# An expert MLP: which engine awaits the ring's stores, and which engine evicts which block of the last expert

## The chip, the core and the metric

The kernel runs on one core of a Trainium2 chip. A core has five engines that run side by side, each with its own instruction stream: TensorE (PE, matrix products), VectorE (DVE), ScalarE (ACT), GpSimd (POOL) and SyncE (SP, which computes nothing and here issues transfers and hands out permissions). They meet only through semaphores: an instruction waits until a semaphore has reached a value, and adds to one when it is done. Transfers between HBM and the on-chip memory are issued by an engine, run on 16 shared DMA engines, and add 16 to a semaphore as they land. TensorE writes its products to PSUM, from where VectorE or ScalarE copy ("evict") them to SBUF.

The metric is the device time of one execution in microseconds. The median of three runs of the kernel before is 181.86 us (181.73 to 181.88).

## The reference

Eight experts, each a two-layer perceptron on 256 rows of its own:

```python
n_experts, capacity, hidden, expert_hidden = 8, 256, 512, 2048
h = np.matmul(x, w1) + b1[:, np.newaxis, :]
h = np.maximum(h, 0)
return (np.matmul(h, w2) + b2[:, np.newaxis, :]).astype(np.float32)
```

x is 8x256x512, w1 8x512x2048, w2 8x2048x512, all float32; the output is 8x256x512 float32.

## The kernel before

The kernel works in float16 with float32 sums. Almost all of it lies in one section whose instruction order and semaphores are written by hand (it opens at line 138 and closes at line 324; the instructions that close it carry line 138 in the profile). Its steps s run from 0 to 10. In step s the first layer of expert s is computed (line 292, hidden units in 16 blocks of 128, each evicted with bias and ReLU by ScalarE, line 226), and the second layer of expert s - 3 (lines 309 and 314: first the bias b2 as a product with a row of ones, then 16 products summed in PSUM). The second layer's 256 rows are two row blocks, tb = 0 and tb = 1, computed one after the other. TensorE adds to `s_po` as each is finished.

`evict(e, tb)` (line 197) copies a finished row block of expert e from PSUM to `results[e]`, and adds to `s_out[tb]`. ScalarE's program (lines 216 to 234) calls it for tb = 0, behind the activations of its step; VectorE's program (lines 210 to 214) calls it for tb = 1, behind the transposes of the next expert's input. For the last expert, E - 1 = 7, in step 10, neither engine has other work left.

The results are stored in three ways:

- Experts 0 to 3 and experts 4 and 5 are stored as two groups by GpSimd, in `flush` (line 165). These are the ring's stores: 2 MB and 1 MB, the last two transfers that GpSimd issues, on the queue on which it also loads all weights. Their landing adds to `landed["out0"]` and `landed["out4"]`.
- Expert 6 is stored by SyncE (line 265) in the last step, between the two permissions for the last expert's weights.
- Expert 7 is stored by SyncE (line 269) when both of its row blocks are evicted (lines 267 and 268). Both of SyncE's stores add to `s_last`.

SyncE's program ends with waiting for the ring's two landings (lines 270 and 271). Then the section is closed: SyncE posts that it has come to the end (line 138), every engine answers with a DRAIN or a NOP and a post, SyncE awaits these and, by a NOP behind the section (line 325), `s_last`, that is, the landing of its own stores. After that the program's end (line 353, where the context that holds the kernel is left) has every engine DRAIN, and all five meet in a barrier that GpSimd opens; a second, short one follows, and the program is over. An engine other than SyncE goes on to its DRAIN of line 353 as soon as it has answered SyncE's post.

Of the kernel before, what the change touches and what calls it, by code (L numbers as in the profile page):

```python
# [10 lines left out]
def kernel(  # L11
# [12 lines left out]
    nc = tc.nc  # L24
# [4 lines left out]
    E, T, H = x.shape  # L29
# [9 lines left out]
    LAG = 3  # L39
    NW = 3  # L40
    NPH = 4
    GROUPS = {0: 4, 4: 2}
# [41 lines left out]
    landed = {}  # L84
# [19 lines left out]
    def transposes(e):  # L104
        t, p0, R = x16[e]
        n = R // nTB
        if e >= 2:
            first = max(f for f in X_LOADS if f <= e)
            nc.vector.wait_ge(landed[f"x{first}"], 16)
            nc.vector.wait_ge(s_ph, nJ * (e - 1))  # L110
        mine = xT[:, e % 2 * nKC * T : (e % 2 + 1) * nKC * T].rearrange("p (kc t) -> p kc t", kc=nKC)
        last = None
        for g in range(T // R // B):
            src = t[p0 + B * g : p0 + B * (g + 1)]
            for b in range(nB):
                block = src[:, :, b * (H // nB) : (b + 1) * (H // nB)].rearrange(
                    "p (n tb) (i kc) -> p tb kc n i", tb=nTB, kc=nKC)
                dst = mine[b * B : (b + 1) * B].rearrange(
                    "p kc (tb g i n) -> p tb g kc n i", tb=nTB, i=B, n=n)
                if n == 1:  # L120
                    last = nc.vector.transpose(out=dst[:, :, g, :, 0, :], in_=block[:, :, :, 0, :])  # L121
                    continue
                for tb in range(nTB):
                    last = nc.vector.transpose(out=dst[:, tb, g], in_=block[:, tb])  # L124
        return last
# [4 lines left out]
        out=b1_rows[:], in_=b1.rearrange("e (b i) -> (e b) i", b=nB)))  # L130
# [59 lines left out]
    for b in range(nB):  # L190
        turned = nc.vector.transpose(  # L191
            out=b1T[b * B : (b + 1) * B, nB - 1 - b : nB - 1 - b + nJ * B],
# [2 lines left out]
    turned.then_inc(s_b1, 1)  # L195

    def evict(e, tb):
        engine = nc.vector if tb else nc.scalar
        copy = nc.vector.tensor_copy if tb else nc.scalar.copy
        first, n = group_of.get(e, (e, 1))  # L200
        rows = P // n
        at = (e - first) * rows
        engine.wait_ge(s_po, nTB * e + tb + 1)
        for k in range(n):
            bank = (e % 2 * nTB + tb) * H
            last = copy(out=results[e][at : at + rows, k * nTB + tb, :],  # L206
                        in_=po[k * rows : (k + 1) * rows, bank : bank + H])
        last.then_inc(s_out[tb], 1)

    for s in range(E + LAG):  # L210
        if s + 1 < E:
            transposes(s + 1).then_inc(s_xT, 1)
        if s >= LAG:
            evict(s - LAG, 1)

    nc.scalar.wait_ge(s_b1, 1)
    for s in range(E + LAG):
        if s < E:
            split = group_of.get(s, (s, 1))[1]
            if s > LAG:  # L220
                nc.scalar.wait_ge(s_po, nTB * (s - LAG))
            for j in range(nJ):
                mine = hT[:, s % (LAG + 1) * nJ * T : (s % (LAG + 1) + 1) * nJ * T]
                bias_at = j * B + s * nB + nB - 1
                nc.scalar.wait_ge(s_ph, nJ * s + j + 1)
                nc.scalar.activation(  # L226
                    out=mine.rearrange("p (tb j k i) -> p j tb k i", tb=nTB, j=nJ, k=split)[:, j],
                    in_=ph[:, j % NPH, 0:T].rearrange("p (tb i k) -> p tb k i", tb=nTB, k=split),
                    func=relu,
                    bias=b1T[:, bias_at : bias_at + 1],  # L230
                    scale=1.0,
                ).then_inc(s_credit, 1)
        if s >= LAG:
            evict(s - LAG, 0)

# [4 lines left out]
    def store(e, p0, p1, engine):  # L242
        dst = out[e].rearrange("(p r) h -> p r h", r=nTB)
        engine.dma_start(out=dst[p0:p1], in_=results[e][p0:p1]).then_inc(s_last, 16)

    for s in range(E + LAG):
# [5 lines left out]
        e = s - LAG  # L252
# [14 lines left out]
    for tb in range(nTB):  # L267
        nc.sync.wait_ge(s_out[tb], E)
    store(E - 1, 0, P, nc.sync)
    for first in GROUPS:  # L270
        nc.sync.wait_ge(landed[f"out{first}"], 16)


    nc.tensor.sem_inc(s_credit, NPH)
# [83 lines left out]
```

## Time and profile before

| what | value |
|---|---|
| time, median of 3 runs | 181.86 us |
| the profiled execution's own time | 182.14 us |
| its span, first to last instruction | 180.4 us |
| TensorE busy (matmul) | 134.9 us, 75% of the span |
| VectorE, ScalarE, GpSimd busy | 86.8, 75.6, 12.5 us |
| mean DMA rate over the span | 224 GB/s |
| granted TensorE clock, mean | 0.970 |

Reading help: PE is TensorE, PEld its weight loads, DVE VectorE, ACT ScalarE, POOL GpSimd, SP SyncE. A "q" behind an engine (SPq, POOLq) marks its sequencer, which handles waits, posts, branches and the issue of transfers; such instructions are not counted as busy. L206 is line 206 of the kernel. "x" before a tile's name, as in `x<-po`, is the tile of the last two experts' results: they lie in buffers that held inputs before. Times in the views are from the start of the span; the views by source line give starts to a tenth of a microsecond and lengths in ns.

### The profile page before, as it was taken

The numbers are of one execution on the slowest core, as the hardware profiler recorded it, in microseconds if no ns is written. First come the engines' busy times: TensorE is split into PE (matmuls) and PEld (weight loads), VectorE is DVE, ScalarE is ACT, GpSimd is POOL, SyncE is SP. The second block draws the span as 40 slices with busy tenths as digits, with TensorE's granted clock in tenths as the row PEclk, the third lists the DMA queues.
The fourth block names the chain that finished last, engine by engine and source line by source line (L and its number), as shares of the span: only waits on it lengthen the run. The fifth ranks groups of instructions, "written<-read, shape, count | busy, mean of one in ns | idle before, by whom it ended". The sixth has DMA issues, their size and how long they took to land. (4 is left out here: it accounts for less than half of the span.)

```text
span 180.4 us, 2999 instructions
## 1 busy us (share of the span) xinstructions
PE 134.9 (75%) x784; PEld 92.5 (51%) x784; DVE 86.8 (48%) x124; ACT 75.6 (42%) x153; POOL 12.5 (7%) x27
## 2 busy tenths in 40 slices
PE   0004969868688970998978896889688979996960
PEld 0003869868688430794378544864388434442320
DVE  1989929585000399996099807990510020201010
ACT  3201777757588040492557352763188010110100
POOL 6000021020200010001010001000200011010000
PEclk9999999999999998599999999999999999999995
DMA  5998999999899999989999999999899999999994
GB/s 229 251 229 180 233 229 205 207 229 227 185 233 202 234 203 233 225 185 229 229 214 196 233 225 203 211 229 225 189 229 229 211 207 215 220 218 172 380 422 169
DMA packets 3826, 40.46 MB, mean 224 GB/s; under 512 B 448, under 2 KB 464, under 8 KB 1392
## 3 DMA queue, kind: packets, MB, share of 16 engines
q0 software_dynamic: 3200, 38.28, 96.2%
q1 hardware_dynamic: 576, 2.10, 2.9%
q10 hardware_dynamic: 48, 0.07, 0.1%
q14 instruction: 2, 0.02, 0.0%
HBM read 71.39 MB, written 4.19 MB: 419 GB/s over the span
## 5 line engine op out<-in xcount | busy, mean ns | idle before, releaser
L292 PE MATMUL ph<-xT,w_sb 128*128 x512 | 72.3, 302 | 33.1 <-PEq L277 30.1
L292 PEld LDWEIGHTS ph<-xT,w_sb 128*128 x512 | 66.7, 146 | 39.7 <-issue 31.0
L226 ACT ACTIVATE hT<-ph,b1T 128x256 f16<-128x256 f32 x128 | 60.2, 475 | 47.1 <-PE ph L292 43.6
L124 DVE STREAM_TRANSPOSE xT<-x 32x256 f16<-32x256 f16 (+1 forms) x64 | 52.8, 893 | 25.2 <-DMA x<-in_x_dram 22.1
L314 PE MATMUL po<-w_sb,hT 128*128 x256 | 58.1, 380 | 0.0
L314 PEld LDWEIGHTS po<-w_sb,hT 128*128 x256 | 24.4, 97 | 29.5 <-issue 4.0
L206 DVE COPY out<-po 32x512 f32<-32x512 f32 (+1 forms) x20 | 13.7, 687 | 42.6 <-PE po L314 42.4
L206 ACT COPY out<-po 32x512 f32<-32x512 f32 (+1 forms) x20 | 11.5, 577 | 28.7 <-PE po L314 28.5
L88 POOL DMA_DIRECT2D w_sb<-in_w_dram x18 | 9.7, 544 | 137.4 <-PE po L314 71.3
L121 DVE STREAM_TRANSPOSE xT<-x 32x256 f16<-32x256 f16 x32 | 14.0, 436 | 0.5
L309 PE MATMUL po<-b_sb,ones 1*128 x16 | 6.1, 383 | 6.2 <-issue 3.6
L206 DVE COPY x<-po 128x512 f32<-128x512 f32 x2 | 1.4, 692 | 15.3 <-PE po L314 15.3
L309 PEld LDWEIGHTS po<-b_sb,ones 1*128 1x128 f16 x16 | 1.4, 90 | 12.0 <-issue 12.0
L206 ACT COPY x<-po 128x512 f32<-128x512 f32 x2 | 1.2, 586 | 15.3 <-PE po L314 15.3
L191 DVE STREAM_TRANSPOSE b1T<-b_rows 32x512 f32<-32x512 f32 x4 | 4.1, 1026 | 0.5 <-issue 0.5
L135 ACT CAST x<-x 128x1024 f16<-128x1024 f32 x1 | 1.0, 1044 | 3.2 <-DMA x<-in_x_dram 3.2
L133 DVE CAST x<-x 128x1024 f16<-128x1024 f32 x1 | 0.7, 695 | 3.0 <-DMA x<-in_x_dram 3.0
L88 POOL DMA_DIRECT2D out_dram<-out x2 | 1.1, 538 | 9.2 <-DVE out L206 9.2
L128 ACT ACT_TABLE_LOAD x1 | 1.3, 1283 | 0.7 <-PEq L342 0.7
L88 POOL DMA_DIRECT2D x<-in_x_dram x2 | 1.1, 550 | 0.0
L127 DVE MEMSET ones<- 1x128 f16 x1 | 0.2, 165 | 0.9 <-PEq L342 0.9
L88 POOL DMA_DIRECT2D b_sb<-in_b_dram x1 | 0.5, 509 | 0.0
(5 smaller groups left out, 0.7 us busy)
## 6 DMA issues: line engine op xcount, KB each, us to landing
w_sb<-in_w_dram POOLq DMA_DIRECT2D x14, 2048.0 KB, 41.2
w_sb<-in_w_dram POOLq DMA_DIRECT2D x2, 1536.0 KB, 22.5
out_dram<-out POOLq DMA_DIRECT2D x1, 2048.0 KB, 25.3
x<-in_x_dram SPq DMA_DIRECT2D x2, 512.0 KB, 3.8
x<-in_x_dram POOLq DMA_DIRECT2D x1, 1024.0 KB, 34.6
w_sb<-in_w_dram POOLq DMA_DIRECT2D x2, 512.0 KB, 24.7
out_dram<-out POOLq DMA_DIRECT2D x1, 1024.0 KB, 18.5
out_dram<-x SPq DMA_DIRECT2D x2, 512.0 KB, 6.6
```

Source lines behind the costliest of these rows:

```text
L88: engine.dma_start(**kw).then_inc(landed[key], 16)
L121: last = nc.vector.transpose(out=dst[:, :, g, :, 0, :], in_=block[:, :, :, 0, :])
L124: last = nc.vector.transpose(out=dst[:, tb, g], in_=block[:, tb])
L128: tc.keep_in_program_order(nc.scalar.activation(out=warm[:], in_=ones1[:], func=relu))
L133: nc.vector.tensor_copy(out=x16[0][0][:], in_=x32[0][:])
L135: tc.keep_in_program_order(nc.scalar.copy(out=x16[1][0][:], in_=x32[1][:]))
L191: turned = nc.vector.transpose(out=b1T[b * B : (b + 1) * B, nB - 1 - b : nB - 1 - b + nJ * B], in_=b1_rows[:].rearrange("r (i j) -> r j i" ...
L206: last = copy(out=results[e][at : at + rows, k * nTB + tb, :], in_=po[k * rows : (k + 1) * rows, bank : bank + H])
L226: nc.scalar.activation(out=mine.rearrange("p (tb j k i) -> p j tb k i", tb=nTB, j=nJ, k=split)[:, j], in_=ph[:, j % NPH, 0:T].rearrange("p ...
L292: last = nc.tensor.matmul(ph[:, j % NPH, 0:T], w1_sb[:, bass.ds(w_from + (kc * M + j), P, nJ)], xT[:, bass.ds(x_at + kc * T, T)], start=(k ...
L309: nc.tensor.matmul(bank, ones1[:], b2_sb[:, bass.ds(s * H, H)], start=True, stop=False)
L314: last = nc.tensor.matmul(bank, hT[:, bass.ds(t * (nJ * P // H) + j * P, P)], w2_sb[:, bass.ds(w_at + j * H, H)], start=False, stop=(j == ...
```

## The change

Two edits. The waits for the ring's two landings move from the end of SyncE's program to the end of ScalarE's. And the last expert's two evictions exchange engines: VectorE copies tb = 0, ScalarE tb = 1; for the other experts nothing changes. SyncE still waits for both row blocks before it stores the last expert.

```diff
     def evict(e, tb):
-        engine = nc.vector if tb else nc.scalar
-        copy = nc.vector.tensor_copy if tb else nc.scalar.copy
+        by_vector = tb == (0 if e == E - 1 else 1)
+        engine = nc.vector if by_vector else nc.scalar
+        copy = nc.vector.tensor_copy if by_vector else nc.scalar.copy
...
         if s >= LAG:
-            evict(s - LAG, 1)
+            evict(s - LAG, 0 if s - LAG == E - 1 else 1)
...
         if s >= LAG:
-            evict(s - LAG, 0)
+            evict(s - LAG, 1 if s - LAG == E - 1 else 0)
+    for first in GROUPS:
+        nc.scalar.wait_ge(landed[f"out{first}"], 16)
...
     store(E - 1, 0, P, nc.sync)
-    for first in GROUPS:
-        nc.sync.wait_ge(landed[f"out{first}"], 16)
```

All instructions keep their place and number on VectorE, GpSimd and TensorE; on ScalarE and SyncE only the two waits before the section's closing branch change sides.

## The prediction

> **What bounds the kernel now.** The change touches the last expert and the end of the program, so I read the chain of waits there first, from 165.9 us on (start, length, work), and beside it the page's first line:
>
> ```profile
> span 180.4 us, 2999 instructions
> ...
> 165.81 0.20 issue
> ...
> 170.62 3.57 PE po L314 x16
> 174.20 0.02 issue
> 174.22 0.69 DVE x L206
> ```
>
> TensorE's matmuls of the last expert's second row block end at 174.20. VectorE's eviction follows until 174.91, and there the chain stops. What fills the 5.5 us to 180.4 is no computing, so the page's shares say nothing about it. I went on with the waits of SyncE from 174 us (total, times, longest):
>
> ```profile
> SPq L268 <- DVE x L206: 6.1, 1, 6.1
> SPq L271 <- DMA out_dram<-out: 2.0, 1, 2.0
> SPq L353 <- PEq L353: 1.5, 2, 1.1
> SPq L138 <- DMA out_dram<-x: 0.7, 1, 0.7
> ```
>
> SyncE (SP) waits for the eviction, then 2.0 us at line 271 for a ring store, then only 0.7 us at line 138 for its own last store. After that it waits once more, for 1.1 us, in the barrier that ends the program (L353). So somebody reaches that barrier 1 us later than SP. The views by source line name it (engine, operation, count, length min/median/max in ns, first and last start):
>
> ```profile
> L271 SPq EVENT_SEMAPHORE  x1: 17/17/17, 177.4 to 177.4; - x1
> ...
> L88 SPq COMPARE_BRANCH  x1: 33/33/33, 177.4 to 177.4; - x1
> ...
> L138 SPq EVENT_SEMAPHORE  x4: 17/22/735, 177.6 to 177.9; - x4
> L138 ACTq DRAIN  x1: 8/8/8, 177.6 to 177.6; - x1
> L138 POOLq NOP  x1: 13/13/13, 177.6 to 177.6; - x1
> ...
> L138 SPq NOP  x1: 13/13/13, 178.7 to 178.7; - x1
> ...
> L353 POOLq DRAIN  x1: 1929/1929/1929, 177.7 to 177.7; - x1
> L353 SPq DRAIN  x1: 7/7/7, 178.8 to 178.8; - x1
> L353 POOLq EVENT_SEMAPHORE  x1: 17/17/17, 179.7 to 179.7; - x1
> ```
>
> The hand-written section is closed at line 138 by a post of SP at 177.6, on which every engine waits. GpSimd (POOL) gets it at 177.6, leaves the section and starts the program's closing DRAIN at 177.7. That takes 1.929 us, to 179.63. SP is ready at 178.8, held to then by the landing of its last store. The barrier therefore opens at 179.7, by POOL's DRAIN, 0.9 us after SP stood there. **The bound of the end is this chain: ring store lands, SP closes the section, POOL drains.** The store of the last expert, which one would suspect, ends 0.9 us too early to matter.
>
> **The change part by part.**
>
> *The waits for the ring stores leave SP.* Two waits and the branch behind them stay in number and go to ScalarE (ACT). The rows of the two issues in question, from the views by line and of transfers:
>
> ```profile
> L244 SPq DMA_DIRECT2D out_dram<-x x1: 344/344/344, 175.0 to 175.0; - x1
> ...
> DMA to landing us min/median/max: 3.6/3.6/3.6
> ...
> 158.83 0.54 POOL L88 DMA_DIRECT2D out_dram<-out  x1 [8.94 <-DVE out L206]
> ...
> out_dram<-out POOLq DMA_DIRECT2D x1, 1024.0 KB, 18.5
> ```
>
> The later ring store lands at 158.83 + 18.5 = 177.3; SP's wait passes it on at 177.4. The last store is issued at 175.0 and lands at 178.6. Without the wait SP goes on after issuing it, at 175.0 + 0.34 = 175.3. From SP's last ring wait to POOL's DRAIN it was 177.4 to 177.7, 0.3 us, so POOL now drains from 175.6; at the same 1.93 us it is done at 177.5. SP is then the last at the barrier, at 178.8, and the barrier opens there and not at 179.7: **0.9 us less**. The tenths leave some 0.1 of doubt. SP's 1.1 us in the barrier check it: after POOL's step at 179.7 SP goes on at about 179.8, which leaves 1.0 that can vanish.
>
> *The DRAIN's price with stores in flight* is what the trace doesn't show: before, both ring stores had landed when it began. The nearest rows are POOL's other DRAINs, at the start of the program with four small fills ahead of it, and after the barrier with nothing ahead:
>
> ```profile
> L342 POOLq DRAIN  x1: 186/186/186, 0.3 to 0.3; - x1
> ...
> L353 POOLq DRAIN  x2: 45/68/90, 179.9 to 180.1; - x2
> ```
>
> So a DRAIN's length depends on what POOL did before, between 0.05 and 1.93 us. Downward nothing is gained: SP arrives at 178.8 anyhow. Upward the cover is 178.8 - 175.6 = 3.2 us; beyond it every microsecond is on the path. The upper end is a DRAIN that starts counting at the landing: 177.33 + 1.93 = 179.26, against 177.7 + 1.93 = 179.63 now, so that only 0.37 is won. I take 1.93 from its start, because in the one case shown it was not waiting for the ring to land: the last landing had been 0.3 us before it. Both ends are kept.
>
> The Trainium skill, "VectorE: DVE Perf Modes", section "The DRAIN you can't avoid", says the closing sequence's DRAINs take about 12 ns, the same on all five engines. SP's and ACT's 7 and 8 ns above agree, POOL's 1929 ns doesn't; by the rule POOL would never be late and the change would be worth no more than its eviction part, some 181.8 us. The row decides against it, so it gets no chance below. The Trainium skill, "Perfetto Trace Analysis", section "DMA Instruction — SWDGE (GPSIMD)", ends GpSimd's own work on a transfer with the writing of its descriptors, ahead of the landing; by it a DRAIN needn't wait for the ring stores. No row here shows whether it does.
>
> *The waits on ACT.* Behind them on ACT stand its line-138 DRAIN and the closing barrier; SP's close waits for that DRAIN's post. ACT would see the landing at 177.4 and post some 0.2 later, as SP did (177.4 to 177.6), so at 177.6. What hides it is the last store, for which SP waits at line 138 until 178.6, 1.0 us longer. Cost nothing; with that cover gone up to 0.2 us, and below nothing isn't possible, since SP needs both anyway.
>
> *The exchanged evictions.* Both forms have rows at the same size (128x512 floats):
>
> ```profile
> L206 ACT COPY x<-po x1: 586/586/586, 170.0 to 170.0; 128x512 f32<-128x512 f32 x1
> L206 DVE COPY x<-po x1: 692/692/692, 174.2 to 174.2; 128x512 f32<-128x512 f32 x1
> ```
>
> VectorE now takes the block that is ready at 170.0 and ends 0.11 us later; SP doesn't need it before 174.8, so 4 us cover that. ACT takes the last block: 692 - 586 = 106 ns earlier, and so the last store's issue. Its landing need not follow. The traffic by queue, two lines for each microsecond from 175, 176 and 177 us (queue, packets, MB, share of the 16 engines; q0 carries the ring stores, q1 SP's), shows why:
>
> ```profile
> q0 software_dynamic: 48, 0.39, 92.7%
> q1 hardware_dynamic: 1, 0.00, 0.1%
> ...
> q1 hardware_dynamic: 53, 0.22, 52.7%
> q0 software_dynamic: 41, 0.21, 51.1%
> ...
> q1 hardware_dynamic: 88, 0.30, 74.3%
> q0 software_dynamic: 1, 0.00, 0.1%
> ```
>
> The transfer engines are full with the ring store for a microsecond after the issue, then share it, then finish q1 alone. Bytes queued at full engines end at the same time whoever starts first; an earlier start helps only where engines stood idle. The bounds are 0 and 0.11 us; I take half, **0.05**. This counts only because SP's landing becomes the bound.
>
> **The sum.** The profiled execution took 182.14 us, 1.74 outside its span of 180.4. 182.14 - 0.9 - 0.05 = 181.19, a span of some 179.45. It stood 0.28 above the median of 181.86, so the forecast is 180.91.
>
> **The rivals.**
>
> *A, the forecast* (0.68): the DRAIN is over before SP's store has landed. Its own range is 180.75 to 181.1: 0.8 to 1.0 from the tenths, 0 to 0.11 from the swap.
>
> *B, the DRAIN waits for POOL's own transfers* (0.13) and takes its 1.93 us from the landing. It ends 0.37 earlier than now: 181.5. For it: it is the only DRAIN here with transfers behind it, and the only long one. Against it: with everything landed it should have had nothing left to wait for.
>
> *C, the DRAIN ends with the core's traffic* (0.11): it ended 1.03 us after the last store's landing at 178.6 and might be tied to that. Then it starts 2 us earlier, grows by 2 us, and only the 0.05 of the swap is left: 181.8. The change would move a wait and nothing else. Against it: SP's store is not in POOL's queue.
>
> *D, slower* (0.08): the DRAIN closes the two ring stores one after another when it finds them unfinished. From 177.4 with 1.93 us each it would end at 181.2, 1.56 after now: 183.4. It decides once the DRAIN is longer than 179.63 - 175.6 = 4.0 us. For it: a length that grows with the work ahead of it, as 0.05, 0.19 and 1.93 show. Against it speaks what POOL had issued before the 1.93 us:
>
> ```profile
> L88 POOL DMA_DIRECT2D w_sb<-in_w_dram x18 | 9.7, 544 | 137.4 <-PE po L314 71.3
> ...
> L88 POOL DMA_DIRECT2D out_dram<-out x2 | 1.1, 538 | 9.2 <-DVE out L206 9.2
> ...
> L88 POOL DMA_DIRECT2D x<-in_x_dram x2 | 1.1, 550 | 0.0
> ...
> L88 POOL DMA_DIRECT2D b_sb<-in_b_dram x1 | 0.5, 509 | 0.0
> ```
>
> If the length went by transfers, 23 of them paid 1.93 us, under 0.1 each, and two left open would not cost 1.93 apiece.
>
> **How the numbers follow.** Shorter than 180.7 needs more than both terms whole; A and B, 0.81 together, lie below 181.6. The range is 180.7 to 181.6. About 0.2% is what a measurement of this kernel can tell from no change, so the line is at 181.5, on which B lies: I split it. Faster is 0.68 + 0.07 = 0.75, the same 0.06 + 0.11 = 0.17, slower 0.08.
>
> **What would show it.** In the changed profile POOL's closing DRAIN should start near 175.5 and still take 1.9 us; B gives one of some 3.7 us, C of 4, D over 4. SP's wait in the barrier should shrink from 1.1 to about 0.1 us, its line-138 waits grow to some 2 us on ACT and 1 us on its store, and the last eviction should read 586 ns on ACT. The store landing at 178.5 or 178.6 tells what the swap was worth. The forecast is wrong if the DRAIN, not SP, still opens the barrier.

## The result, and the profile after

| | before | changed |
|---|---|---|
| median of 12 runs each | 181.89 us | 181.02 us |
| ratio | | 0.9956, 95% interval 0.9935 to 0.9977 |
| profiled execution, its span | 182.14, 180.4 us | 180.79, 179.0 us |

The change made the kernel faster by 0.4% (0.2 to 0.65%); the medians are 0.87 us apart. It was forecast at 180.91, in a range of 180.7 to 181.6.

The waits of SyncE in the changed profile, from 172 us on (total, times, longest), answer to the four rows shown of before:

```profile
SPq L271 <- ACT x L207: 6.2, 1, 6.2
SPq L138 <- ACTq L138: 1.9, 1, 1.9
SPq L138 <- DMA out_dram<-x: 1.0, 1, 1.0
SPq L354 <- PEq L354: 0.6, 2, 0.4
```

The wait for the ring's store has become a wait for ScalarE's answer at the section's close, 1.9 us. Behind it stands the last store's landing for 1.0 us, as long as was forecast. In the barriers of the program's end (now line 354) SyncE's two waits together fall from 1.5 to 0.6 us; the longest of 0.4 is the second, short barrier. The views by source line of the same profile show who opens the first one:

```profile
L237 ACTq EVENT_SEMAPHORE  x1: 17/17/17, 176.9 to 176.9; - x1
...
L138 POOLq NOP  x1: 13/13/13, 175.1 to 175.1; - x1
...
L354 SPq DRAIN  x2: 7/7/7, 178.3 to 178.3; - x2
L354 POOLq DRAIN  x1: 2741/2741/2741, 175.1 to 175.1; - x1
...
L354 POOLq EVENT_SEMAPHORE  x1: 17/17/17, 178.3 to 178.3; - x1
...
L207 DVE COPY x<-po x1: 691/691/691, 170.1 to 170.1; 128x512 f32<-128x512 f32 x1
L207 ACT COPY x<-po x1: 585/585/585, 174.0 to 174.0; 128x512 f32<-128x512 f32 x1
...
L247 SPq DMA_DIRECT2D out_dram<-x x1: 344/344/344, 174.6 to 174.6; - x1
...
DMA to landing us min/median/max: 3.5/3.5/3.5
```

GpSimd leaves the section at 175.1 and not at 177.6. Its DRAIN is over at 175.14 + 2.74 = 177.88, 0.46 us before the barrier opens at 178.34. What opens it is SyncE, whose store landed at 178.13. But the DRAIN did not keep its length: it is 2741 ns long and was 1929.

Where the 1.35 us between the two profiled spans went, by the trace's instants: the barrier opened 1.09 us after the last store's landing (178.604 to 179.694) and now 0.21 us after it (178.132 to 178.343), which is 0.88. The last store landed 4.41 us after the last product was ready (174.196) and now 4.19 (173.943): 0.22. This is not the work of the exchanged evictions: in the profiles of the two parts alone, below, the same stretch is 4.40 us with the exchange and 4.16 without it. The last product itself was ready 0.25 us earlier; nothing ahead of it was changed, and the runs of one kernel differ by more.

### The profile page after: what moved, and what is told of

Its sections match the earlier page's. It is cut to its first block, busy times and chain, and to the rows that moved or that the text cites. A ratio compares the mean times of both kernels' runs of the same rounds, so it can differ in the third digit from the quotient of the medians.

```text
span 179.0 us, 2999 instructions
## 1 busy us (share of the span) xinstructions
PE 135.3 (76%) x784; PEld 92.5 (52%) x784; DVE 86.7 (48%) x124; ACT 75.2 (42%) x153; POOL 12.5 (7%) x27
## 3 DMA queue, kind: packets, MB, share of 16 engines
HBM read 71.39 MB, written 4.19 MB: 422 GB/s over the span
```

## The experiments

Nine kernels were run. A table at the end of this section gathers what is used throughout: when the ring's later store landed, when GpSimd's closing DRAIN began, and its length.

**One part alone: the waits.** Only the ring's waits go to ScalarE; the evictions stay as before.

```diff
         if s >= LAG:
             evict(s - LAG, 0)
+    for first in GROUPS:
+        nc.scalar.wait_ge(landed[f"out{first}"], 16)
...
     store(E - 1, 0, P, nc.sync)
-    for first in GROUPS:
-        nc.sync.wait_ge(landed[f"out{first}"], 16)
```

> The ring's waits go to ScalarE, the evictions stay as before. Theory (the barrier was held by GpSimd's closing DRAIN, which waited for SyncE's post): nearly the whole gain is here, DRAIN from about 175.5, the barrier opened by SyncE some 0.2 us after the last store's landing, time 0.8 to 0.9 us below before (181.0 to 181.1). Rival (the gain came from the exchanged evictions or from the work ahead of them): no gain over 0.3 us, 181.6 or more.

Measured: 181.02 us, ratio to before 0.9946 (0.9926 to 0.9966). The closing rows of its profile:

```profile
L353 SPq DRAIN  x2: 7/7/7, 178.5 to 178.5; - x2
L353 POOLq DRAIN  x1: 2607/2607/2607, 175.5 to 175.5; - x1
...
L353 POOLq EVENT_SEMAPHORE  x1: 17/17/17, 178.6 to 178.6; - x1
```

The barrier opens when SyncE arrives, 0.21 us after its store's landing. The waits alone carry the whole gain.

**The other part alone: the evictions.** The evictions exchange engines as in the change; the ring's waits stay on SyncE. Against the changed kernel:

```diff
             evict(s - LAG, 1 if s - LAG == E - 1 else 0)
-    for first in GROUPS:
-        nc.scalar.wait_ge(landed[f"out{first}"], 16)
...
     store(E - 1, 0, P, nc.sync)
+    for first in GROUPS:
+        nc.sync.wait_ge(landed[f"out{first}"], 16)
```

> The evictions exchange engines, the ring's waits stay on SyncE. Theory: the last store is issued 0.1 us earlier, but the ring's landing still holds SyncE's post and GpSimd's DRAIN still opens the barrier, so time as before within 0.1 us (181.8 to 181.9). Rival (the eviction carries the gain): 0.3 us or more below before.

Measured: 181.90 us, ratio 1.0000 (0.9988 to 1.0013). The DRAIN is back at 1929 ns from 177.5, and GpSimd opens the barrier at 179.5, with SyncE there at 178.6 already:

```profile
L354 SPq DRAIN  x2: 7/7/7, 178.5 to 178.6; - x2
...
L354 POOLq DRAIN  x1: 1929/1929/1929, 177.5 to 177.5; - x1
...
L354 POOLq EVENT_SEMAPHORE  x1: 17/17/17, 179.5 to 179.5; - x1
```

**SyncE free, but GpSimd late.** As the changed kernel, with the ring's waits at the end of GpSimd's program.

```diff
     for first in GROUPS:
         flush(first)
+    for first in GROUPS:
+        nc.gpsimd.wait_ge(landed[f"out{first}"], 16)
...
-    for first in GROUPS:
-        nc.scalar.wait_ge(landed[f"out{first}"], 16)
```

> As the changed kernel, but the ring's waits stand at the end of GpSimd's own program and not ScalarE's. SyncE is as free as in the changed kernel. Theory (what counts is when GpSimd's DRAIN starts): it starts 0.2 to 0.3 us after the ring's landing again and takes 1.9 us, the barrier opens by it, time as before (181.7 to 182.0). Rival (what counts is that SyncE no longer waits): as the changed kernel, 181.0.

Measured: 181.80 us, ratio 0.9998 (0.9987 to 1.0009): the whole gain is gone, though SyncE, once it has issued the last store, is held by nothing but that store's landing.

```profile
L187 POOLq EVENT_SEMAPHORE  x1: 17/17/17, 177.0 to 177.0; - x1
...
L354 SPq DRAIN  x2: 7/7/7, 178.3 to 178.4; - x2
L354 POOLq DRAIN  x1: 1929/1929/1929, 177.3 to 177.3; - x1
L354 POOLq EVENT_SEMAPHORE  x1: 17/17/17, 179.3 to 179.3; - x1
```

What matters is when GpSimd begins to drain, not what SyncE is spared.

**What the DRAIN waits for.** ScalarE issues the last store itself, so that SyncE closes the section over 6 us earlier.

```diff
+    for tb in range(nTB):
+        nc.scalar.wait_ge(s_out[tb], E)
+    store(E - 1, 0, P, nc.scalar)
     for first in GROUPS:
         nc.scalar.wait_ge(landed[f"out{first}"], 16)
...
-    for tb in range(nTB):
-        nc.sync.wait_ge(s_out[tb], E)
-    store(E - 1, 0, P, nc.sync)
```

> As the changed kernel, but ScalarE issues the last store itself behind its eviction, so that SyncE posts the section's end about 6 us earlier, near 169, with both ring stores and the last store still to land. Theory 1 (the DRAIN has a length of its own, up to 2.7 us with stores in flight): it starts near 169 and is over by 172. Theory 2 (the DRAIN waits for the ring's landing and then takes 1.0 us, as in the changed profile): it ends near 177.9, about 8.8 us long. In both the last store's landing opens the barrier, so the time is that of the changed kernel or up to 0.1 us less (180.9 to 181.0).

Measured: 180.82 us, ratio 0.9945 (0.9924 to 0.9965), the same as the changed kernel within the noise. The row that decides:

```profile
L355 POOLq DRAIN  x1: 9392/9392/9392, 168.5 to 168.5; - x1
...
L355 POOLq EVENT_SEMAPHORE  x1: 17/17/17, 178.4 to 178.4; - x1
...
L245 ACTq EVENT_SEMAPHORE  x1: 17/17/17, 177.0 to 177.0; - x1
```

The DRAIN began at 168.5 and ended at 177.94, 0.98 us after the ring's landing. Theory 2 holds: with transfers of GpSimd in flight the DRAIN waits for them, and then takes 0.98 us more. The same 0.98 stands in the changed profile and in that of the waits alone.

**Whose transfers.** The ring's stores are issued by SyncE, once the last weights have landed, so that GpSimd has nothing of its own in flight when it drains.

```diff
     def flush(first):
...
-            nc.gpsimd.wait_ge(s_out[tb], first + n)
-        load(nc.gpsimd, f"out{first}", in_=results[first][:],
+            nc.sync.wait_ge(s_out[tb], first + n)
+        load(nc.sync, f"out{first}", in_=results[first][:],
...
     tc.wait_critical_data_deps()
-    for first in GROUPS:
-        flush(first)
...
             go(f"w2_{e}_{FIRST}", 2 * nTB - 1)
+    for first in GROUPS:
+        flush(first)
     for tb in range(nTB):
         nc.sync.wait_ge(s_out[tb], E)
```

> As the changed kernel, but the two ring stores are issued by SyncE, on its queue, once the last weights have landed (about 168.4), so that every transfer that GpSimd issued has landed when it drains (about 175.5 or later) while 3 MB of stores on another queue still move. Theory 2a (the DRAIN waits for GpSimd's own transfers alone): 1.93 us, as where the ring had landed. Theory 2b (it waits for whatever the core still moves, or the traffic slows it): it ends about 1.0 us after the ring's landing, 2.5 us or longer. The time is no test: the stores start later, 181 to 184 us.

Measured, in one execution: 181.06 us, and a DRAIN that ended at 176.84, before the ring's landing at 177.15 (line 272 is ScalarE's wait for it):

```profile
L354 POOLq DRAIN  x1: 1766/1766/1766, 175.1 to 175.1; - x1
...
L272 ACTq EVENT_SEMAPHORE  x1: 17/17/17, 177.2 to 177.2; - x1
```

So it does not wait for SyncE's transfers, only for GpSimd's own. (GpSimd's are also the only ones on the software queue q0; whether the engine or the queue decides is not told apart here.) Theory 2a was right on what is waited for, but neither theory had 1766 ns: it is 163 less than 1929, and GpSimd had issued 21 transfers and not 23. A loss of time from the later stores is not seen in this one execution.

**The DRAIN with nothing in flight.** SyncE awaits its own stores before it closes the section.

```diff
     store(E - 1, 0, P, nc.sync)
+    nc.sync.wait_ge(s_last, 16 * len(HALVED))
```

> As the changed kernel, but SyncE awaits the landing of its own stores before it posts the section's end, so that GpSimd drains with nothing in flight at all, from about 178.4. If 1.93 us is the DRAIN's fixed price where all own transfers have landed: 1.93 us again, the barrier opens near 180.4, about 2 us above the changed kernel (182.9 to 183.1). If the last store in flight had lengthened it before: 1.0 us or so, about 182.1.

Measured, in one execution: 183.47 us; the DRAIN takes 1929 ns again.

```profile
L355 SPq DRAIN  x2: 7/7/7, 179.3 to 179.4; - x2
...
L355 POOLq DRAIN  x1: 1929/1929/1929, 179.0 to 179.0; - x1
...
L355 POOLq EVENT_SEMAPHORE  x1: 17/17/17, 181.0 to 181.0; - x1
```

From the store's landing (178.753) to the barrier (181.022) it is 2.27 us, in the changed kernel 0.21: the 2 us expected. The time lies 0.4 above the forecast, and this execution's store landed 0.62 later than in the changed profile. The DRAIN takes 1929 ns here with nothing in flight, and took the same in the kernel before with SyncE's last store still in flight: that store did not lengthen it.

**Does an earlier start of the last store help?** It goes in two halves, one for each row block; `s_last` counts three stores in place of two.

```diff
     for tb in range(nTB):
         nc.sync.wait_ge(s_out[tb], E)
-    store(E - 1, 0, P, nc.sync)
+        nc.sync.dma_start(
+            out=out[E - 1].rearrange("(p r) h -> p r h", r=nTB)[:, tb],
+            in_=results[E - 1][:, tb]).then_inc(s_last, 16)
```

> As the changed kernel, but the last expert's store goes in two halves, one row block each: the first 3.3 us earlier, 256 KB and not 512 KB left behind the last eviction. In the six profiles so far the last store landed 1.23 us after the ring's landing, whenever it was issued. Theory (the transfer engines are full to the end, so the queued bytes set the end): the last landing moves by less than 0.2 us, time as the changed kernel within 0.2 us. Rival (the 3.5 us from the last issue to its landing is the store's own length): 0.5 us or more less, 180.5.

Measured: 181.17 us, ratio 0.9954 (0.9928 to 0.9980), the changed kernel's within the noise. The two issues, the closing DRAINs and the ring's landing:

```profile
L272 SPq DMA_DIRECT2D out_dram<-x x2: 332/338/344, 170.8 to 174.6; - x2
...
DMA to landing us min/median/max: 3.8/5.4/7.0
...
L356 SPq DRAIN  x2: 7/7/7, 178.5 to 178.6; - x2
L356 POOLq DRAIN  x1: 3508/3508/3508, 175.1 to 175.1; - x1
...
L237 ACTq EVENT_SEMAPHORE  x1: 17/17/17, 177.6 to 177.6; - x1
```

Half the bytes left 3.9 us earlier than in the changed kernel and took 7.0 us, and the ring landed at 177.62, 0.7 later than there. The second half, with half the bytes, took 3.8 us. The last landing stands 4.45 us behind the last product, no better than 4.19. The rival is out: the store's 3.5 us are not its own length. The DRAIN, 0.98 us behind the ring's later landing, ended at 178.60 here, level with SyncE: the cover was used up. By these rows a last store that landed still earlier would gain nothing unless the ring's stores landed earlier too.

**The DRAIN's price by the transfer.** The kernel before, with the load of b2 cut into eight: 30 transfers of GpSimd.

```diff
-    load(nc.gpsimd, "b2", out=b2_sb[:, LAG * H :],
-         in_=b2.rearrange("e h -> (e h)").rearrange("(o f) -> o f", o=1))
+    landed["b2"] = sem("d_b2")
+    for e in range(E):
+        nc.gpsimd.dma_start(out=b2_sb[:, (LAG + e) * H : (LAG + e + 1) * H],
+                            in_=b2[e : e + 1, :]).then_inc(landed["b2"], 16)
...
-            nc.sync.wait_ge(landed["b2"], 16)
+            nc.sync.wait_ge(landed["b2"], 16 * E)
```

> The kernel before with its load of b2 cut into eight, so that GpSimd issues 30 transfers and not 23; waits and evictions as before. GpSimd's closing DRAIN took 1929 ns with 23 transfers behind it and 1766 ns with 21 (all landed): 81.5 ns each. Theory (the DRAIN is paid by the transfer): 1929 + 7 x 81.5 = 2500 ns, the barrier opens 0.57 us later, time 0.5 to 0.6 us above before (182.4 to 182.5). Rival (a fixed price; the 163 ns had another cause, such as the two large stores): 1929 ns, time as before.

Measured: 182.56 us, where before, measured beside it, had a median of 181.92; the ratio is 1.0019 (0.9992 to 1.0047), so the times alone can't tell it from no change. The profile is sharper:

```profile
L355 SPq DRAIN  x2: 7/7/7, 179.1 to 179.2; - x2
...
L355 POOLq DRAIN  x1: 2501/2501/2501, 178.1 to 178.1; - x1
...
L355 POOLq EVENT_SEMAPHORE  x1: 17/17/17, 180.7 to 180.7; - x1
```

and, from SyncE's waits in the same profile:

```profile
SPq L355 <- PEq L355: 2.0, 2, 1.6
```

The DRAIN takes 2501 ns against 2500 forecast, SyncE stands 1.6 us in the barrier and not 1.1, and the barrier opens 1.65 us after the last store's landing and not 1.09. The changed kernel with the same seven transfers more:

> The changed kernel with the same seven more transfers. Its DRAIN ended 0.98 us after the ring's landing in four profiles, however early it began. If it waits in the middle of walking through the transfers, at the one still in flight, the part behind that is either as long as before (0.98 us; end as in the changed kernel) or longer by up to 0.57 us (1.55 us, then it ends about when SyncE arrives). In both SyncE's arrival or nearly that opens the barrier, so the time is that of the changed kernel within 0.2 us: what costs 0.57 us before costs nothing here.

Measured: 181.07 us, ratio 0.9939 (0.9913 to 0.9965).

```profile
L356 SPq DRAIN  x2: 7/7/7, 179.2 to 179.2; - x2
L356 POOLq DRAIN  x1: 3226/3226/3226, 175.8 to 175.8; - x1
...
L239 ACTq EVENT_SEMAPHORE  x1: 17/17/17, 177.8 to 177.8; - x1
```

The DRAIN ends at 179.07, 1.27 us behind the ring's landing and 0.16 before SyncE. The changed kernel hides the seven transfers too, with little to spare. The part behind the landing grew by 0.29, neither 0 nor 0.57.

All of it in one table, by the trace's instants (us):

| kernel | transfers of GpSimd | ring landed | DRAIN from | its length | its end after the landing |
|---|---|---|---|---|---|
| before | 23 | 177.366 | 177.721 | 1.929 | landed already |
| evictions alone | 23 | 177.182 | 177.537 | 1.929 | landed already |
| waits on GpSimd | 23 | 176.982 | 177.315 | 1.929 | landed already |
| late close | 23 | 177.519 | 179.049 | 1.929 | landed already |
| changed | 23 | 176.898 | 175.138 | 2.741 | 0.981 |
| waits alone | 23 | 177.136 | 175.511 | 2.607 | 0.982 |
| last store split | 23 | 177.622 | 175.095 | 3.508 | 0.981 |
| early close | 23 | 176.958 | 168.548 | 9.392 | 0.982 |
| ring on SyncE | 21 | 177.153, not GpSimd's | 175.072 | 1.766 | it doesn't wait |
| 30 transfers, waits as before | 30 | 177.765 | 178.120 | 2.501 | landed already |
| 30 transfers, waits as changed | 30 | 177.797 | 175.839 | 3.226 | 1.268 |

No version beats the changed kernel by more than the runs scatter.

## Why the prediction was right, and where not

*What bounded the end* was read rightly: the chain from the ring's landing over SyncE's post to GpSimd's DRAIN. Putting the waits on GpSimd keeps that chain and loses everything; a later post costs 2 us; a DRAIN longer by 0.57 us in the kernel before opens the barrier 0.56 later.

*The moved waits, 0.9 us:* right, 0.88 in the profiles, and the waits alone give it. The DRAIN began at 175.1, half a microsecond before the 175.6 that was worked out. The last store's issue came some 0.36 earlier in this profile, and the 0.3 us taken over from the chain before held a pause of 0.12 behind SyncE's branch that didn't recur: SyncE posted 0.04 after its store's issue.

*The DRAIN's price with stores in flight* is the step that failed. "I take 1.93 from its start" was wrong: it took 2.74. The reason given, that it "was not waiting for the ring to land" in the one case shown, proved nothing, because there was nothing left to wait for. Nor did the DRAIN keep any length of its own: it ended 0.98 us behind the ring's landing. Rival B had the mechanism, waiting for GpSimd's own transfers, and was given 0.13; its own price was wrong in the other direction, 1.93 us behind the landing where 0.98 was measured. With 1.93 the DRAIN would have ended at 178.83, where the barrier opened at 178.34, and the time would have been near B's 181.5. The forecast held because 2.74 lies inside the cover of 3.2 us that had been worked out beside the price. That it lies inside was luck: nothing in the prediction said that what follows the landing takes 0.98 us and not 1.93, and 0.46 us were to spare.

A page was cited there by which the DRAIN needn't wait: the Trainium skill, "Perfetto Trace Analysis", section "DMA Instruction — SWDGE (GPSIMD)". It describes the transfer's own instruction, and the runs show that nothing about a DRAIN follows from it: 9.39 us with the ring in flight, 1.77 with the same bytes on another engine's queue.

*Rivals C and D* fall. C tied the DRAIN's end to the core's traffic: the changed kernel's DRAIN ended 0.25 us before the last landing. D wanted 1.93 us for each store left open: the argument against it, that a transfer cost under 0.1 us, was right: 81.5 ns each.

*The waits on ScalarE, nothing:* right; SyncE's wait for ScalarE's answer ended at 177.17, 0.96 us before the store landed.

*The exchanged evictions, 0.05 us:* not seen, and too small for the times to tell. ScalarE did take 585 ns. That the exchange alone gives 1.0000 is no test of the 0.05, which was to count only where the landing of SyncE's store is the bound; where it is, the changed kernel and the waits alone, 0.9956 and 0.9946, can't be told apart. The profiles say more. In the nine in which the ring is GpSimd's and the last store goes in one piece, that store was issued between 2.1 and 2.5 us before the ring's landing and landed 1.23 to 1.25 us after it, whichever engine evicted. The reason given, full transfer engines, fits, and taken to its end it would have given 0.

## What to carry to other kernels

Read the end of a kernel past its last computing instruction: here the order in which engines were let go there cost 0.9 us of 181.9. An engine with a long closing step (here GpSimd, by the number of its transfers) should be let into it before its last transfers land; still earlier brought nothing here, since the step waits for them (9.39 us long in the early close, at the changed kernel's time). Waits for landings belong on an engine that has little to close, here ScalarE. A price that is unknown can be left open if the cover is worked out, but then from the event on which the step hangs: here not from the DRAIN's start, but from the ring's landing.

## What the runs showed of the hardware

GpSimd's DRAIN at the program's end costs by the transfer, even where all have long landed: 1766, 1929 and 2501 ns for 21, 23 and 30 transfers, which is 55 + 81.5 ns times their number to within 1 ns. The first two lengths give both figures, and the third was forecast from them. The other engines' DRAINs of the same closing lines took 7 to 19 ns.

If some of these transfers are still in flight, it waits for them and then takes half of that price again: 0.98 us with 23 transfers (half of 1.929 is 0.965) and 1.27 with 30 (half of 2.501 is 1.25), both some 0.02 above the half. That would fit two passes over the transfers, of which the first, or its end, has to see all landed; the passes themselves are not shown.
